# Products that pile up in PSUM, VectorE for the late remainders, and additions made by the DMA queue, in a hybrid decoder layer

## The chip, the core and the metric

The kernel runs on one core of one Trainium2 chip. The core has a matrix engine (TensorE: PE in the profile for its matmuls, PEld for the loads of its weights), a vector engine (VectorE: DVE), an engine for activations and copies (ScalarE: ACT), a general engine (GpSimd: POOL), and a queue engine (SyncE: SP) that issues the DMAs. Matmuls add into PSUM, a small memory in banks of 128 partitions x 512 float32; everything else works on SBUF, 128 partitions wide. The metric is the device time of one execution in microseconds (us), lower is better.

## The reference

One decoder layer for 1024 tokens and a width of 1024, all in float32: a norm, one wide projection that feeds two branches (sliding-window attention with 16 heads, and gated linear attention with 4 heads), each branch gated and projected, the two results merged with sigmoid gates, one output projection, the residual, and a norm at the end.

```python
h = rms_norm(x, norm_w)
z = h @ w_in                      # q, k, v, gates of both branches, merge gates m_a, m_b
o_a = sliding_window_attention(...) * silu(gate_a)
o_b = rms_norm(gated_linear_attention(...)) * silu(gate_b)
y = sigmoid(m_a) * (o_a @ w_a_proj) + sigmoid(m_b) * (o_b @ w_b_proj)
out = rms_norm(x + y @ w_out, final_norm_w)
```

## The kernel before, in words

**Float32 on a matrix engine that takes less.** Every operand of a matmul is held in two parts of the reduced format fp32r: the rounded value `h` and the remainder `l`. A product of two operands is three matmuls, h·h + h·l + l·h. For weights, `split_w` (L114-116) makes `h` by a copy on ACT (L115) and `l` by a subtraction on POOL (L116). For data, `split_block` (L878-880) makes `h` on ACT (L879) and `l` on DVE, or on POOL where the caller says so (L880).

**Seven products instead of eight.** A 1024-deep product is cut into 2 x 2 blocks and computed by Winograd's form of Strassen's scheme, `seven_products` (L398-463): seven half products of sums of the blocks of weights (a11, a12, a21, a22) with sums of the blocks of data (b11, b21, t4, t2, t3, t1, b22), and then additions of the seven results into the four blocks of the output. We call the products by their factors: P1 = a11·b11, P2 = a12·b21, P3 with t2, P4 with t1, P5 with t3, P6 with t4, P7 with b22. Each product has PSUM banks of its own, and DVE does the additions: seven for every output tile (L426, L436, L462). Before P3, four subtractions on DVE make the sums of the weights (L454-457), and each of the seven weights goes through `split_w`.

**Stages.** Norm and transposes of x (to about 100 us of the profiled span); the projections for the merge gate m_b, for q, k, v and the gate of the linear branch, in pairs of 128 or 256 columns through `seven_products` (100 to 440); the attention (440 to 740); the linear branch together with the remaining projections, and the projection of the first branch, `ya`, whose gated result t1 goes to HBM as `sp_t1` (740 to 922); then the **end stage**, in which the second branch is projected and merged, and the layer's output is made.

**The end stage.** The output of the second branch, `sp_ob`, is loaded (tiles `r`) and turned into the seven data blocks `ob` (`b0` to `b9` and `o0` to `o3`, each an `h` and an `l`). Four steps k = 0 to 3 follow, each a `seven_products` of 7 x 12 matmuls of 128x512 with a pair of column blocks of `w_b_proj`; `merge` takes each of the four output tiles c11, c12, c21, c22, multiplies it by the gate (L957), and adds the part of the first branch that it loads from `sp_t1` (tile `yt`, L958). The sixteen merged tiles stay in SBUF (`mg`). When all four steps are through, `block_sums` makes the seven data blocks of the merged result, `mt`: 16 sums on DVE (L891-L898) and 28 splits. Of the splits' remainders DVE takes those of blocks 2 and 3, POOL those of blocks 0, 1, 4, 5 and 6. The output projection is two `seven_products` with n = 256 (h = 0 and 1, each half of the 1024 output columns), 7 x 48 matmuls of 128x256 each (L395). `residual` loads the piece of x that belongs to a tile (`xr`) and DVE adds it (L1000); `norm` has ACT sum the squares (L1007), and POOL multiply by the final norm's weight (L1011). At the very end `finish` scales by the root and stores.

**What sets the order.** The program states what depends on what. A scheduler that simulates a timeline then puts each engine's instructions into one fixed list. An engine takes its own list in order: an instruction that waits holds up all that stand behind it on that engine. Names with a number in the listings below are tiles; a tile that reuses the space of another one waits for it.

Of the kernel before, what the change touches and what calls it, by code (L numbers as in the profile page):

```python
# [69 lines left out]
def layer_kernel(ctx: ExitStack, tc: tile.TileContext, consts, x, positions, norm_w, w_in, a_sinks,  # L70
# [42 lines left out]

    def split_w(raw, h, l):  # L114
        nc.scalar.copy(h, raw)  # L115
        nc.gpsimd.tensor_sub(l, raw, h.bitcast(F32))  # L116
# [10 lines left out]
    def half_product(p, w, m, start, stop):  # L127

        for k in range(4):
            with tc.issue_after(pace.pop(0)) if pace else nullcontext():  # L130
                for y, (a, b) in enumerate(((w[0], m[0]), (w[0], m[1]), (w[1], m[0]))):
                    nc.tensor.matmul(p, a[:, k, :], b[:, k, :], start=start and k == 0 and y == 0,  # L132
                                     stop=stop and k == 3 and y == 2)
# [257 lines left out]
    def token_product(p, w, m, t):  # L391

        for k in range(4):
            for y, (i, j) in enumerate(((0, 0), (1, 0), (0, 1))):
                nc.tensor.matmul(p, m[i][:, k, t * P : t * P + P], w[j][:, k, :], start=k == 0 and y == 0,  # L395
                                 stop=k == 3 and y == 2)

    def seven_products(raw, tset, n, u_pool, dest, emit, early=None, fine=False):  # L398
# [7 lines left out]

        def product(raw, m):
            w = part(raw, n)
            x = [bank("sj") for b in range(nb)]
            for b in range(nb):  # L410
                if n == P:
                    half_product(x[b], w, m, True, True)
                else:
                    for t in range(2):
                        token_product(x[b][:, t * 256 : t * 256 + 256], w, m, 2 * b + t)
            return x

        def tiles(name):
            return [u_pool.tile([P, 512], F32, name=name) for b in range(nb)]
# [4 lines left out]
        def add(o, u, x):  # L424
            for b in range(nb):
                nc.vector.tensor_add(o[b], like(u[b], o[b]), like(x[b], o[b]))  # L426

        def earlier(u, a, th):
            for b in range(nb):
                if early:  # L430
                    early(u[b], a, th, b)

        def give(a, th, u, x):
            o = [dest(a, th, b) for b in range(nb)]
            for b in range(nb):
                nc.vector.tensor_add(o[b], like(u[b], o[b]), like(x[b], o[b]))  # L436
                emit(o[b], a, th, b)

        x = product(a11, b11)
        u = tiles("u")  # L440
        for b in range(nb):
            nc.scalar.copy(u[b], x[b])
        x = product(a12, b21)
        c = [dest(0, 0, b) for b in range(nb)]
        add(c, u, x)
        earlier(c, 0, 0)
# [595 lines left out]
```

## Time and profile before

| | |
|---|---|
| three timed runs | 1125.82, 1119.82, 1123.76 us (median 1123.76) |
| the profiled execution's own time | 1122.67 us |
| its span, and what lies around it | 1120.8 us, 1.87 us |
| matmuls in the profile | 5544 |
| mean granted clock of TensorE | 0.969 |
| end stage: from the last matmul of `ya` to the last matmul | 921.85 to 1111.4 us |
| after the last matmul | 9.4 us |

Busy time is the sum of the durations of an engine's instructions. Where an engine idles, the profile names what ended the wait ("releaser"). The start-to-start time of two instructions that follow each other is called pitch here: it is what one more instruction of a kind costs an engine that never waits, and it is shorter than an instruction's own duration, since neighbours overlap.

### The profile page before, as it was taken

Reading aid. Unit: us, or ns where it says so; the run is one execution under the profiler, and the core shown is the slowest. Engines: PE = TensorE matmul, PEld = TensorE weight load, DVE = VectorE, ACT = ScalarE, POOL = GpSimd, SP = SyncE. Lnnn points to the kernel's source line nnn. Section 1 sums busy time; section 2 is a strip of 40 time slices with the busy share of each in tenths; the row PEclk is TensorE's granted clock in tenths of the full one; section 3 lists DMA queues with packets and bytes.
Section 4 is the critical chain, followed back from the end, with each engine's and each line's share of the span. In section 5 each row is a group of like instructions: output and inputs, shape, how many; then the busy total and the mean of one; then the engine's idle time right before and its main releaser. Section 6 shows DMA issues by size and latency. Waiting matters only on the chain.

```text
span 1120.8 us, 16315 instructions
## 1 busy us (share of the span) xinstructions
PE 1035.0 (92%) x5544; PEld 877.8 (78%) x5544; DVE 765.8 (68%) x1225; ACT 542.4 (48%) x1312; POOL 705.5 (63%) x558
## 2 busy tenths in 40 slices
PE   4797999989999999999999999988999998994896
PEld 3575878868889997888888888776788876874896
DVE  6894687554565422378888888748765199899766
ACT  6326576333343222466666665647554144243444
POOL 4544555677788354867677768548735244688685
PEclk8998999999999999999999999999899998997999
DMA  6303433544333325212222223356644587531315
GB/s 230 95 29 118 149 124 123 169 136 150 101 113 105 112 75 133 72 46 82 67 83 71 64 67 103 109 196 227 197 144 155 167 264 251 180 113 56 121 50 188
DMA packets 126403, 141.07 MB, mean 126 GB/s; under 512 B 10352, under 2 KB 87024, under 8 KB 126320
## 3 DMA queue, kind: packets, MB, share of 16 engines
q1 hardware_dynamic: 126320, 140.03, 39.7%
q8 instruction: 44, 0.72, 0.3%
q14 instruction: 39, 0.32, 0.1%
HBM read 95.04 MB, written 40.24 MB: 121 GB/s over the span
## 4 chain that ended last, share of the span: by engine, by line
PE 57%; DVE 14%; POOL 10%; issue 6%; DMA 5%; ACT 5%; SPq 2%; POOLq 0%; DVEq 0%; ACTq 0%
PE sj L132 21%; PE pj L132 15%; PE sj L395 11%; POOL wl L116 3%; POOL b L880 2%; PE av L748 2%; PE av L703 1%; PE sc L663 1%; DMA r<-sp_ob 1%; POOL o L880 1%; DVE qa L643 1%; ACT sm L678 1%; POOL q L585 1%; DMA oraw<-sp_oa 1%; PE sc L748 1%
## 5 line engine op out<-in xcount | busy, mean ns | idle before, releaser
L132 PE MATMUL pj<-o,wh 128*128 128x512 f32 x1088 | 357.9, 404 | 10.4 <-DVE low L308 6.0
L132 PEld LDWEIGHTS pj<-o,wh 128*128 128x128 f32 x1088 | 203.5, 192 | 53.7 <-issue 6.4
L116 POOL TENSOR_TENSOR wl<-wr,wh 128x1024 fp32r<-128x1024 f32 (+1 forms) x76 | 166.9, 2206 | 98.0 <-ACT wh L115 85.9
L132 PE MATMUL pj<-o,wl 128*128 128x512 f32 x544 | 217.6, 400 | 0.0
L116 POOL TENSOR_TENSOR wl<-sraw,wh 128x512 fp32r<-128x512 f32 (+1 forms) x98 | 152.6, 1574 | 90.6 <-ACT wh L115 80.9
L132 PEld LDWEIGHTS pj<-o,wl 128*128 128x128 f32 x544 | 103.9, 191 | 22.1
L132 PE MATMUL sj<-o,wh 128*128 128x512 f32 x352 | 112.0, 399 | 4.8 <-ACT wh L115 4.8
L115 ACT CAST wh<-wr 128x1024 fp32r<-128x1024 f32 (+1 forms) x76 | 67.0, 890 | 92.1 <-PE pj L132 24.4
L426 DVE TENSOR_TENSOR u<-u,sj 128x512 f32<-128x512 f32 x72 | 49.2, 684 | 74.2 <-PE sj L395 38.3
L115 ACT CAST wh<-sraw 128x512 fp32r<-128x512 f32 (+1 forms) x98 | 63.3, 678 | 63.3 <-PE sj L395 27.9
L132 PEld LDWEIGHTS sj<-o,wh 128*128 128x128 f32 x352 | 66.7, 190 | 21.5 <-ACT wh L115 5.1
L395 PE MATMUL sj<-wh,b 128*128 128x256 f32 x320 | 62.5, 297 | 21.4 <-ACT b L879 14.4
L395 PEld LDWEIGHTS sj<-wh,b 128*128 128x128 f32 x320 | 53.0, 204 | 22.8 <-ACT b L879 14.8
L132 PE MATMUL sj<-o,wl 128*128 128x512 f32 x176 | 70.1, 398 | 0.0
L695 POOL TENSOR_TENSOR ch<-ph,cst 128x512 fp32r<-128x512 f32 x32 | 38.4, 1199 | 46.9 <-ACT ph L694 34.4
L678 ACT ACTIVATE sm<-sc,nm 128x129 f32<-128x129 f32 x128 | 45.8, 368 | 36.7 <-DVE nm L674 35.6
L132 PE MATMUL sj<-b,wh 128*128 128x512 f32 x160 | 51.4, 405 | 4.3 <-ACT wh L115 4.3
L395 PE MATMUL sj<-wh,o 128*128 128x256 f32 x320 | 55.2, 277 | 0.1
L395 PEld LDWEIGHTS sj<-wh,o 128*128 128x128 f32 x320 | 48.4, 188 | 0.4 <-ACT wh L115 0.3
L395 PE MATMUL sj<-wl,b 128*128 128x256 f32 x160 | 45.9, 294 | 0.2 <-POOL wl L116 0.2
L395 PE MATMUL sj<-wl,o 128*128 128x256 f32 x160 | 44.2, 277 | 0.0
L583 POOL TENSOR_TENSOR qs<-qs,sin 128x512 f32<-128x512 f32 x18 | 25.0, 1391 | 30.3 <-DMA qs<-q 30.3
(313 smaller groups left out, 2748.7 us busy)
## 6 DMA issues: line engine op xcount, KB each, us to landing
sraw<-in_w_in_dram SPq DMA_DIRECT2D x32, 512.0 KB, 4.0
wr<-in_w_in_dram SPq DMA_DIRECT2D x26, 512.0 KB, 3.9
r<-sp_ob SPq DMA_DIRECT2D x28, 256.0 KB, 4.5
qs<-q SPq DMA_DIRECT2D x72, 64.0 KB, 2.0
xt<-in_x_dram SPq DMA_DIRECT2D x8, 512.0 KB, 8.7
sp_ma<-gt SPq DMA_DIRECT2D x16, 256.0 KB, 2.0
sp_mb<-c SPq DMA_DIRECT2D x16, 256.0 KB, 2.0
gt<-sp_cum SPq DMA_DIRECT2D x16, 256.0 KB, 3.8
```

The costliest lines, as they stand in the source:

```text
L115: nc.scalar.copy(h, raw)
L116: nc.gpsimd.tensor_sub(l, raw, h.bitcast(F32))
L132: nc.tensor.matmul(p, a[:, k, :], b[:, k, :], start=start and k == 0 and y == 0, stop=stop and k == 3 and y == 2)
L395: nc.tensor.matmul(p, m[i][:, k, t * P : t * P + P], w[j][:, k, :], start=k == 0 and y == 0, stop=k == 3 and y == 2)
L426: nc.vector.tensor_add(o[b], like(u[b], o[b]), like(x[b], o[b]))
L583: nc.gpsimd.tensor_mul(qs, qs, sin[:, sl])
L585: nc.gpsimd.tensor_add(q, q, qs)
L643: nc.vector.tensor_sub(qa[64:128, :], r[0:64, :], qa[0:64, :].bitcast(F32))
L678: nc.scalar.activation(sm[:, j, :], sel[j // 2][:, j % 2, :], AF.Exp, bias=nm[:, j : j + 1], accum_out=den[:, j : j + 1])
L695: nc.gpsimd.tensor_mul(ch, ph.bitcast(F32), leb)
L748: nc.tensor.matmul(p, a[i], b[j], start=start and y == 0, stop=stop and y == 2)
L880: (eng or nc.vector).tensor_sub(m[1][:, k, :], r, f(m, 0, k))
```

## The change

- **`seven_products` is rewritten.** P3 and P5 are added by TensorE onto the banks in which P1 stands, P7 onto the banks of P4. After P1, after P3 and after P5, ACT copies the bank out (tiles u1, u3, u5). DVE has four additions for each output tile (`give`, L433 of the changed kernel): c11 = u1 + P2, c22 = u5 + P4, c21 = u5 + P6, c12 = u3 + (P4 + P7). Nothing is added into the bank of P4 until c22 has read it. The weights a11, a12 and a22 are split ahead of the four subtractions. The order of the products is an argument: 1 to 7, or for n = 256 (1, 2, 6, 3, 5, 4, 7) and in the first half of the output projection (1, 2, 4, 6, 3, 5, 7).
- **Remainders.** From the projection of the first branch's fourth column block on, `split_w` makes `l` on DVE (`rest[0] = nc.vector`). All remainders of data blocks and the multiplication by the norm's weight go from POOL to DVE too.
- **Sums earlier.** `block_sums` is gone. The last two of the second branch's data blocks are made between the products of step k = 0, and the seven blocks of the merged result between the products of step k = 3 (`sums`): the parts of k = 0, 1, 2 first, and those of k = 3 as their tiles come.
- **Additions by DMA.** In `merge`, for k < 3, a DMA issued by GpSimd adds `sp_t1` into the tile in SBUF (twelve of 256 KB, L976); for k = 3 the load and DVE's addition stay. The residual is added in the same way for the whole first half and for two of four tile groups of the second (twelve of 256 KB, L1021).
- **Places.** The halves of `w_out`'s rows are exchanged together with the data blocks; some pools lie elsewhere, t2 shares the tiles `r`, and the memory for the queue of GpSimd's DMAs is set to 1024.

```diff
+    rest = [nc.gpsimd]
+
     def split_w(raw, h, l):
         nc.scalar.copy(h, raw)
-        nc.gpsimd.tensor_sub(l, raw, h.bitcast(F32))
+        rest[0].tensor_sub(l, raw, h.bitcast(F32))
...
+        w = {i: part(r, n) for i, r in ((1, a11), (2, a12), (6, a22))}
         nc.vector.tensor_add(a22, a21, a22)
         nc.vector.tensor_sub(a21, a11, a21)
         nc.vector.tensor_sub(a11, a22, a11)
         nc.vector.tensor_sub(a12, a12, a11)
+        by = {1: (b11, a11), 2: (b21, a12), 3: (t2, a11), 4: (t1, a22), 5: (t3, a21), 6: (t4, a22), 7: (b22, a12)}
...
+        def product(i, b):
+            if n == P:
+                half_product(x[i][b], w[i], by[i][0], i not in (3, 5, 7), i not in (1, 3, 4))
...
+        for i in order:
+            if i not in w:
+                w[i] = part(by[i][1], n)
+            x[i] = x[{3: 1, 5: 1, 7: 4}[i]] if i in (3, 5, 7) else [bank("sj") for b in range(nb)]
...
+            if i in (1, 3, 5):
+                u[i] = [u_pool.tile([P, 512], F32, name=f"u{i}") for b in range(nb)]
+                for b in range(nb):
+                    nc.scalar.copy(u[i][b], x[i][b])
+                    if i == 3 and early:
+                        early(u[i][b], 0, 1, b)
+            if i == 2:
+                give(0, 0, 1, 2)
+            if i in (4, 5) and 4 in x and 5 in u:
+                give(1, 1, 5, 4)
+            if i in (5, 6) and 6 in x and 5 in u:
+                give(1, 0, 5, 6)
+            if i == 7:
+                give(0, 1, 3, 7)
+            if after:
+                after(i)
...
     ya_tiles((0, 1, 2))
+    rest[0] = nc.vector
...
             nc.vector.scalar_tensor_tensor(o, m, 1.0, o, ALU.add, ALU.mult)
-            nc.vector.tensor_add(o, o, t)
+            if k < 3:
+                nc.gpsimd.dma_start(o, sp_t1[c : c + P, sl], accum_op=ALU.add)
+            else:
+                t = yw.tile([P, 512], F32, name="yt")
+                nc.sync.dma_start(t, sp_t1[c : c + P, sl])
+                nc.vector.tensor_add(o, o, t)
...
-    block_sums(mt, [(k, [mg[i][th][:, k, :] for i in range(2) for th in range(TH)]) for k in range(4)], zw, (0, 1, 4, 5, 6))
...
-            nc.vector.tensor_add(u, u, xr)
+            if h == 0 or (a, th) in ((0, 0), (0, 1)):
+                nc.gpsimd.dma_start(u, xs, accum_op=ALU.add)
+            else:
+                xr = zw.tile([P, 2, 256], F32, name="xr")
+                nc.sync.dma_start(xr, xs)
+                nc.vector.tensor_add(u, u, xr)
...
-                    nc.gpsimd.tensor_mul(o[:, t, :], o[:, t, :], fnw[:, cs])
+                    nc.vector.tensor_mul(o[:, t, :], o[:, t, :], fnw[:, cs])
```

The instruction lists show what this moves. The first place is POOL, from the projections of the end stage to the first tiles of the output. Before (`wl` is a weight's remainder, the tiles `b_...` and `o_...` on the left are remainders of the blocks `mt`, `o_10208` a tile of the output):

```order
L116 TENSOR_TENSOR wl<-wr,wh 128x512 x26
L880 TENSOR_TENSOR b_10119<-o_9490,b_10118 128x512 x3
L880 TENSOR_TENSOR b_10121<-o_9492,b_10120 128x512 x3
L880 TENSOR_TENSOR b_10119<-o_9490,b_10118 128x512
L116 TENSOR_TENSOR wl<-wr,wh 128x1024 x2
L880 TENSOR_TENSOR b_10127<-o_9491,b_10126 128x512 x3
L880 TENSOR_TENSOR o_10129<-o_9490,o_10128 128x512 x3
L880 TENSOR_TENSOR b_10121<-o_9492,b_10120 128x512
L116 TENSOR_TENSOR wl<-wr,wh 128x1024
L880 TENSOR_TENSOR o_10131<-o_9493,o_10130 128x512 x4
```

After, from the last three tiles of step k = 2 on (`o_9381` to `o_9384` are the merged tiles c11, c12, c21 and c22; `u_...` and `o_10104` on belong to the output):

```order
L976 DMA o_9384<-sp_t_78 128x512
L976 DMA o_9383<-sp_t_78 128x512
L976 DMA o_9382<-sp_t_78 128x512
L1021 DMA o_10104<-in_x_dram 128x2x256 x2
L1021 DMA u_10411<-in_x_dram 128x2x256
L1021 DMA u_10412<-in_x_dram 128x2x256
L1021 DMA o_10105<-in_x_dram 128x2x256
L1021 DMA o_10104<-in_x_dram 128x2x256
```

Nine more lines of the first kind stand ahead of these, and five of the second behind. POOL's subtractions and multiplications are gone from its list in the end stage; what stands there is the issue of 24 DMAs, and at the very end the roots of the final norm.

The second place is DVE, from the last tile of step k = 3 to the sums. Before (`o_9490` to `o_9493` are the merged tiles, `t_...` and `b_...` sums and remainders for the output projection):

```order
L436 TENSOR_TENSOR o_9491<-u,sj 128x512
L957 SCALAR_TENSOR_TENSOR o_9491<-ym,o_9491 128x512
L958 TENSOR_TENSOR o_9491<-o_9491,yt 128x512
L893 TENSOR_TENSOR t_10149<-o_9493,o_9490 128x512
L891 TENSOR_TENSOR o_9490<-o_9491,o_9490 128x512
L894 TENSOR_TENSOR o_9492<-o_9492,t_10149 128x512
L898 TENSOR_TENSOR o_9491<-o_9493,o_9491 128x512
L880 TENSOR_TENSOR b_10125<-t_10149,b_10124 128x512
L880 TENSOR_TENSOR b_10123<-o_9492,b_10122 128x512
L893 TENSOR_TENSOR t_10157<-o_9493,o_9490 128x512
```

After, in the same place (`b_9891`, `b_10046` and `o_10080` are remainders of blocks that go into the output projection, `u_9944` is the copy of P3; the additions that give c21 and c22 of k = 3 stand ten rows higher):

```order
L433 TENSOR_TENSOR o_9382<-u_9944,sj 128x512
L866 TENSOR_TENSOR b_10046<-o_9381,b_10045 128x512
L980 TENSOR_TENSOR o_9384<-o_9384,yt 128x512
L118 TENSOR_TENSOR wl<-wr,wh 128x1024
L866 TENSOR_TENSOR o_10080<-o_9382,o_10079 128x512
L980 TENSOR_TENSOR o_9383<-o_9383,yt 128x512
L866 TENSOR_TENSOR o_10080<-o_9382,o_10079 128x512
L974 SCALAR_TENSOR_TENSOR o_9382<-ym,o_9382 128x512
L866 TENSOR_TENSOR o_10080<-o_9382,o_10079 128x512
L412 TENSOR_TENSOR wr<-wr 128x1024
L866 TENSOR_TENSOR b_9891<-o_9383,b_9890 128x512
L980 TENSOR_TENSOR o_9382<-o_9382,yt 128x512
```

Additions out of PSUM, gates, remainders of blocks, sums, and remainders and sums of the weights of the output projection now stand mixed in one list. TensorE's list changes with it: 37 matmuls of the output projection's first two products stand ahead of step k = 3's last product.

The third place is the first tile group of the output, on DVE after the change (`fnw` is the norm's weight, `o_10104` the tile into which the DMA of L1021 adds):

```order
L433 TENSOR_TENSOR o_10104<-u_10185,sj 128x2x256
L433 TENSOR_TENSOR o_10104<-u_10186,sj 128x2x256
L866 TENSOR_TENSOR b_9947<-r,b_9946 128x512
L866 TENSOR_TENSOR b_10015<-o_9384,b_10014 128x512
L866 TENSOR_TENSOR b_10046<-o_9381,b_10045 128x512
L118 TENSOR_TENSOR wl<-wr,wh 128x1024
L1038 TENSOR_TENSOR o_10104<-o_10104,fnw 128x256 x4
L118 TENSOR_TENSOR wl<-wr,wh 128x1024 x2
```

The multiplications of L1038 stand behind the DMAs that add x into the same tile, and two weight remainders stand behind them in the list.

221 lines of the change are left out of this document (103 added, 118 removed).

## The prediction

> **What bounds the kernel now.** I read the page's busy list and its chain first, then the busy time by stage, then what TensorE waited for in the end stage, and last the rows around each wait.
>
> ```profile
> span 1120.8 us, 16315 instructions
> PE 1035.0 (92%) x5544; PEld 877.8 (78%) x5544; DVE 765.8 (68%) x1225; ACT 542.4 (48%) x1312; POOL 705.5 (63%) x558
> PE 57%; DVE 14%; POOL 10%; issue 6%; DMA 5%; ACT 5%; SPq 2%; POOLq 0%; DVEq 0%; ACTq 0%
> ```
>
> TensorE is busy 92% of the span, so only its idle or slow stretches can be won, and the number of its matmuls does not change. By stage (columns: PE, PEld, DVE, ACT, POOL busy with instructions, granted clock, DMA share, GB/s):
>
> ```profile
> 100.00:440.00 340.00, 334.69 (x1761) 285.37 (x1762) 177.90 (x224) 141.74 (x222) 218.12 (x143) 0.99 0.40 126
> 921.85:1004.08 82.23, 77.92 (x329) 63.30 (x328) 75.80 (x86) 30.47 (x52) 53.58 (x35) 0.96 0.62 193
> 1004.08:1050.23 46.15, 24.39 (x155) 22.70 (x153) 43.60 (x40) 17.40 (x29) 33.76 (x18) 0.78 0.13 40
> 1050.23:1111.40 61.17, 61.16 (x518) 60.97 (x518) 41.42 (x58) 27.51 (x76) 49.98 (x43) 1.00 0.38 126
> 1111.40:1120.80 9.40, 0.00 (x0) 0.00 (x0) 3.52 (x12) 3.68 (x8) 3.03 (x7) 0.73 0.60 223
> ```
>
> The hole is 1004 to 1050 us, the hand-over from the second branch's projection to the output projection: 24.39 us busy of 46.15, clock 0.78. From 1050 on TensorE is the bound again, at 61.17 / 518 = 0.118 us per 128x256 matmul. The waits from 880 us on (total, times, longest) and two rows of the chain (start, length):
>
> ```profile
> PE sj L395 <- ACT b L879: 14.4, 2, 12.6
> PE sj L395 <- DVE b L880: 4.8, 2, 3.6
> PE sj L132 <- ACT wh L115: 4.3, 1, 4.3
> PE sj L395 <- DVE u L426: 2.2, 1, 2.2
> PE sj L395 <- POOL wl L116: 0.2, 1, 0.2
> ...
> 925.46 4.97 DMA r<-sp_ob
> 932.69 54.86 PE sj L132 x227
> ```
>
> and TensorE's timeline after the first of these waits (start, length, operation, idle before it):
>
> ```profile
> 932.69 2.08 PE L132 MATMUL sj<-b,wh 128*128 128x512 f32 x4 [4.31 <-ACT wh L115]
> 938.31 0.40 PE L132 MATMUL sj<-b,wl 128*128 128x512 f32 x1
> ```
>
> Thirteen matmuls take the 5.62 us between these two rows; in the chain's run of 227, with the excess taken off, one takes (54.86 - 2.6) / 227 = 0.23, and 13 would be 3.0. So a long wait costs 2.6 us more in slow clock. The end stage after `ya` runs from 921.85 to 1111.40, 189.55 us. Its matmuls alone, 334 of 128x512 and 672 of 128x256, need 334 x 0.23 + 672 x 0.118 = 156.1. **Lost: 33.4 us** = 4.3 + 2.6 at the start, 21.6 of waits in the hand-over (14.4 + 4.8 + 2.2 + 0.2), and the remaining 4.9 in slow clock there. Nothing outside of this is large: the pairs stage, with 334.69 busy of 340.00, can give 5.3 at most.
>
> **The change, part by part.**
>
> *Start of the second branch's projection.* ACT's weight copy stood behind a data split that waited for a load of 4.97 us. The last two data blocks now come inside step k = 0, so the weight copy stands ahead of them, and the wait moves to P4, which needs a block whose loads are queued on SP behind the last stores of `ya`. My walk gives 1.5 us there, between 0 (loads early) and 3 (a load of 4.97 begun two microseconds before it is needed). In place of 6.9: **-5.4**.
>
> *The hand-over.* Before, the sums and splits for the output projection were done by POOL and DVE after the last step. What they cost, and how they slow each other (groups of the end stage from 880 us: busy, mean ns; then DVE's timeline with and without POOL beside it):
>
> ```profile
> L116 POOL TENSOR_TENSOR wl<-wr,wh 128x512 fp32r<-128x512 f32 x28 | 44.4, 1603 | 33.6 <-ACT wh L115 27.6 <-DMA sp_t<-yt 4.9 <-DMA ym<-sp_mb 1.1
> L116 POOL TENSOR_TENSOR wl<-wr,wh 128x1024 fp32r<-128x1024 f32 x16 | 42.6, 2672 | 29.6 <-ACT wh L115 29.6
> L880 POOL TENSOR_TENSOR b<-o,b 128x512 fp32r<-128x512 f32 x12 | 20.6, 1741 | 0.0
> L1011 POOL TENSOR_TENSOR o<-o,fnw 128x256 f32<-128x256 f32 x24 | 21.9, 937 | 2.8 <-ACT zj L1007 2.8
> L958 DVE TENSOR_TENSOR o<-o,yt 128x512 f32<-128x512 f32 x16 | 19.5, 1218 | 0.7 <-DMA yt<-sp_t 0.4
> L442 ACT COPY u<-sj 128x512 f32<-128x512 f32 x8 | 4.7, 584 | 3.5 <-PE sj L395 3.2 <-PE sj L132 0.3
> ...
> 1030.35 1.75 DVE L880 TENSOR_TENSOR b<-o,b 128x512 fp32r<-128x512 f32 x1
> 1032.02 1.76 DVE L893 TENSOR_TENSOR t<-o,o 128x512 f32<-128x512 f32 x1
> 1035.19 0.69 DVE L880 TENSOR_TENSOR b<-o,b 128x512 fp32r<-128x512 f32 x1
> 1035.80 0.69 DVE L893 TENSOR_TENSOR t<-o,o 128x512 f32<-128x512 f32 x1
> 1036.52 0.69 DVE L894 TENSOR_TENSOR o<-o,t 128x512 f32<-128x512 f32 x1
> 1044.32 1.28 DVE L426 TENSOR_TENSOR o<-u,sj 128x512 f32<-128x512 f32 x2
> 1045.51 1.22 DVE L457 TENSOR_TENSOR wr<-wr 128x1024 f32<-128x1024 f32 x1
> 1046.65 1.28 DVE L1000 TENSOR_TENSOR o<-o,xr 128x512 f32<-128x512 f32 x2
> ```
>
> Beside POOL's subtractions a DVE addition starts every 1.67 us (1030.35 to 1032.02). Alone, the pitch is 0.61 for 128x512 (1035.19 to 1035.80), 0.72 where the next one needs the result (1035.80 to 1036.52), and 1.14 for 128x1024 (1045.51 to 1046.65). So taking some 1.7 to 2.7 us of POOL's time off per remainder costs DVE 0.6 to 1.14, and frees DVE's other rows of their slow pace. DVE still has more to do in one place. I walk both lists from t0, the moment at which TensorE ends P5 of step k = 2. By the lists DVE does 60 operations of 128x512 and 4 of 128x1024 from there to the remainder of block b11's part of k = 3 (`b_9891`), the last thing that the first product of the output projection needs: 60 x 0.60 + 4 x 1.14 = 40.6. Its head waits for ACT's copy of P5 (0.58 by the row of L442 above) and its end takes 0.69: 41.9, and my walk, with a short wait for a later product between, has 42.4. TensorE's list to the same place holds 98 matmuls of 128x512 and 80 of 128x256: 98 x 0.23 + 80 x 0.118 = 31.9. It therefore loses 10.5 us on the way, however the waits are spread, and by my walk 0.9 at two later splits: 11.4. One long wait costs 2.6 of clock on top: 14.0 in place of 21.6 + 4.9 = 26.5: **-12.5**. After that 491 matmuls are left, 58 us, in which DVE has about 44 us of work at the same pitches: TensorE is the bound.
>
> *DVE's dependent rows.* The walk used the pitch of independent rows. If a third of its 64 rows wait for the one ahead, 0.11 each: **+2.5**; 0 if the list is mixed well, 7 if all are.
>
> *Additions by DMA.* Twelve additions of L958 (1.2 us each) and twelve of L1000 leave DVE, and SP's loads go with them; those additions are already out of the count above. No DMA issued by POOL, and none that adds, is in the trace. The nearest rows are loads of the same size on SP's queue (KB, us to landing) and, from above, a load of twice the size with much else under way:
>
> ```profile
> yt<-sp_t SPq DMA_DIRECT2D x16, 256.0 KB, 3.7
> xr<-in_x_dram SPq DMA_DIRECT2D x16, 256.0 KB, 3.0
> r<-sp_ob SPq DMA_DIRECT2D x28, 256.0 KB, 4.5
> xt<-in_x_dram SPq DMA_DIRECT2D x8, 512.0 KB, 8.7
> ```
>
> A plain load could be issued early; an addition cannot begin until its tile is multiplied by the gate, so its whole latency lies between that row and the tile's first reader. Two places are tight. For c21 of k = 2, nine DVE rows cover it, 9 x 0.60 = 5.4. For the first tile of the output, three rows and a 128x1024 cover two such DMAs, 2.9, and L1038's four multiplications wait for them with the next weights' remainders behind them; those have some 5 us before TensorE wants them. At 3.0 to 4.5 nothing of it reaches TensorE but the second of two in a row; I take 4.5 and **+1.5**. At 8.7 it is 3.3 at the first place, 0.8 at the second and about 1 at each of two later tiles, +6; below there is nothing to gain.
>
> The Trainium skill ("DMA: Bandwidth & Descriptors", section Anatomy of one DMA) gives for a DMA issued from GpSimd about 2.0 us plus the bytes over 436 KB per us, an estimate of 2.6 us for 256 KB, less than every row above; by it this term would be 0 and the time 1107; no row shows such a DMA.
>
> *The pairs stage.* Of seven DVE additions per tile four are left, 24 tiles in the whole program: 72 of 0.69 us fewer, and 24 ACT copies more. DVE is busy 177.90 of 340 us there and ACT 141.74, so TensorE hides both. New are three waits per pair: P3, P5 and P7 write onto banks that ACT or DVE must have read. One product of twelve matmuls (12 x 0.23 = 2.8 us) stands between each reader and its writer, and a copy and an addition take 0.6 + 0.69 = 1.3. Cost **0**, between -5.3 (the stage's holes vanish, since DVE has fewer rows) and the rival below.
>
> *Tail.* The 9.40 us behind the last matmul keep their last product, addition, squares, root and stores: 0.
>
> Sum against the profiled execution: 1122.67 - 5.4 - 12.5 + 2.5 + 1.5 = 1108.8, **1109 us**. That execution is 1.1 below the median of the runs shown, less than their spread.
>
> **The rivals.**
>
> *DVE keeps ahead (1095).* The scheduler's list for DVE may start earlier than my t0 in its cheap parts, and hide the 10.5. Then only the start's 1.5 and the DMAs' 1.5 are left of 33.4, and some 2 of clock: 1122.67 - 33.4 + 5 = 1094. For it: POOL no longer slows DVE, and DVE is busy only 75.80 of 82.23 us before the hole even at the slow pace. Against: 64 rows stand between two fixed points, and none of them is idle time.
>
> *The shared banks bite in the pairs stage (1123).* ACT and DVE take their lists in order; where a weight's copy (0.62) and a 128x512 sum at 1.67 beside POOL, which in this stage keeps its remainders, stand ahead of the reader, 1.3 becomes 3.6, and the writer waits 0.8 to 1. One such wait in each of 14 pairs is 14 us: 1109 + 14 = 1123. For it: POOL is busy 218.12 of 340 there. Against: ACT is busy 42% and DVE 52%, and the lists I walked for three pairs leave 1 to 5 us of slack.
>
> *The DMAs that add land late (1131).* Mechanism: an ACT or DVE instruction that reads the tile stands in the list and holds up the weights' parts behind it. From 12 us on it decides: 12 - 5.4 = 6.6 for c21 of k = 2, 12 - 2.9 - 5 = 4.1 for the first output tile, and about 4 at each of three later tiles, 22.7 in place of 1.5: 1109 + 21 = 1130 to 1131, slower than before. For it: each is one transfer of 128 rows that has to read, add and write, and all share one queue. Against: 3.0 to 4.5 for the plain ones, and 0.13 of DMA share in the hand-over.
>
> The Trainium skill ("SBUF — State Buffer", "Who interferes with whom") warns that DMAs issued from GpSimd starve while DVE runs some operations, because their descriptors cannot be written; it takes additions of two SBUF tensors out of that, by inference. DVE's list in this place is of such additions, so by the exception nothing happens, and by the warning this rival's 1131 would come. No row of this trace decides it.
>
> **How the numbers follow.** What a measurement of this kernel can tell from no change is about 0.5%: under 1118.1 is faster, over 1129.4 slower. The forecast, DVE bounding the hand-over, 1102 to 1118: 0.55. DVE ahead, 1090 to 1102: 0.12. Pairs stage, 1115 to 1129: 0.20, of which 0.07 under 1118. Late DMAs: 0.13, of which 0.10 above 1129.4. Faster 0.55 + 0.12 + 0.07 = 0.74; slower 0.10 and 0.01 for both losses together, 0.11; same 0.15. The range leaves out 0.07 below and 0.12 above: 1094 to 1126. Its upper end is 1109 plus 4.5 for dependent rows, 4.5 for DMAs at 8.7 and 8 of the pairs' 14; its lower end the first rival.
>
> **What would show it.** In the changed profile: a wait of 1 to 3 us, not 4.3, where the second branch's projection starts; waits on DVE remainders (`b`, `wl`) of 10 to 13 us in all around step k = 3's last product and the start of the output projection, where 21.6 stood, and the stretch from `ya`'s last matmul to the last matmul of all at about 175 us; DVE rows at 0.6 to 0.7 with POOL quiet; DMAs from POOL that land in 3 to 5 us; 100 to 440 us within 2 us of its old length. I am wrong if POOL's DMAs show more than 8 us, if TensorE's waits in the pairs stage name `u` or `c` in many small pieces, or if the hand-over holds no wait on DVE above 2 us.

## The result, and the profile after

The changed kernel takes **1132.55 us** in the median (1131.14 to 1134.62), the kernel before beside it 1124.05: a ratio of 1.0078, 95% interval 1.0051 to 1.0106. It is slower by 0.8%, where 1109 was forecast, with a range of 1094 to 1126. The profiled execution took 1131.14 us, with these lines on its page (span; busy time; share of the chain that ended last; then GpSimd's DMA queue, with packets, MB and share):

```profile
span 1129.4 us, 16128 instructions
PE 1046.2 (93%) x5544; PEld 881.4 (78%) x5544; DVE 705.4 (62%) x1224; ACT 557.2 (49%) x1340; POOL 568.9 (50%) x487
PE 42%; DVE 17%; issue 14%; POOL 9%; DMA 8%; ACT 6%; SPq 1%; POOLq 0%; DVEq 0%; ACTq 0%
...
q0 software_dynamic: 4992, 6.29, 3.6%
```

The work went where the change sends it: POOL 705.5 to 568.9 us, DVE 765.8 to 705.4 although it took over POOL's remainders, ACT 15 more. But the chain's share of TensorE fell from 57 to 42%, and "issue" rose from 6 to 14%. By stage:

```profile
100.00:440.00 340.00, 333.45 (x1741) 279.69 (x1742) 139.15 (x176) 153.66 (x240) 206.64 (x140) 0.99 0.39 124
925.15:1003.00 77.85, 74.79 (x316) 59.34 (x315) 57.43 (x94) 32.11 (x59) 9.79 (x11) 0.98 0.67 176
1003.00:1042.00 39.00, 29.43 (x183) 27.15 (x182) 39.00 (x57) 16.87 (x26) 2.12 (x2) 0.82 0.31 87
1042.00:1120.05 78.05, 66.77 (x508) 65.10 (x507) 38.40 (x70) 30.60 (x83) 17.24 (x21) 0.91 0.45 98
1120.05:1129.40 9.35, 0.04 (x1) 0.00 (x0) 3.54 (x12) 3.52 (x8) 3.20 (x7) 0.78 0.62 228
```

The hand-over (1003 to 1042) is better than it was, with DVE busy 39.00 of 39.00 us: it bounds this stretch, as forecast. The stretch after it is new. Before, 518 matmuls filled 61.17 us without a gap; here 508 take 78.05 with a clock of 0.91. TensorE's timeline in it:

```profile
1054.99 0.80 PE L397 MATMUL sj<-wh,b 128*128 128x256 f32 x2 [3.90 <-ACT u L447]
1085.22 0.80 PE L397 MATMUL sj<-wh,b 128*128 128x256 f32 x2 [4.76 <-ACT wh L117]
1102.23 0.50 PE L397 MATMUL sj<-wh,o 128*128 128x256 f32 x2 [1.44 <-ACT wh L117]
```

Each names a copy on ACT. ACT itself stood behind squares (L1034) that waited for the residual DMAs, on its timeline:

```profile
1047.79 0.42 ACT L1034 ACTIVATE zj<-o 128x256 f32<-128x256 f32 x1 [6.95 <-DMA o<-in_x_dram]
...
1052.47 0.42 ACT L1034 ACTIVATE zj<-o 128x256 f32<-128x256 f32 x1 [3.62 <-DMA o<-in_x_dram]
```

And POOL, which only issues them (start, length, idle before it):

```profile
971.88 1.74 POOL L976 DMA_DIRECT2D o<-sp_t  x2 [7.61 <-DVE o L974]
...
1039.62 1.23 POOL L1021 DMA_DIRECT2D o<-in_x_dram  x1 [34.34 <-issue]
1048.11 1.22 POOL L1021 DMA_DIRECT2D o<-in_x_dram  x1 [7.25 <-issue]
...
1065.93 1.20 POOL L1021 DMA_DIRECT2D o<-in_x_dram  x1 [3.30 <-DVE wl L118]
1070.41 1.22 POOL L1021 DMA_DIRECT2D o<-in_x_dram  x1 [3.29 <-issue]
1075.01 1.20 POOL L1021 DMA_DIRECT2D o<-in_x_dram  x1 [3.39 <-issue]
1079.46 1.22 POOL L1021 DMA_DIRECT2D o<-in_x_dram  x1 [3.25 <-issue]
```

The second residual DMA is ready with the first, at 1039.5 us (both tiles came from one pair of DVE additions), and is issued at 1048.11, just after the first has landed and ACT starts on it (1047.79). Later ones follow each other at 4.5 us, just over the 4.2 us that each of them takes to land; the first took 8.1. The merge's DMAs were issued two at a time (971.88, x2). Something lets one residual DMA at a time through. The residual DMA has 256 rows of 1 KB where the merge's has 128 of 2 KB, and the change gave the memory for this queue the number 1024.

To compare stretches I add up by how much each row of TensorE's timeline starts later than the one ahead allows (0.228 us for each 128x512 matmul, 0.1135 for each 128x256; only excesses over 0.15 us): waits and slow clock together, called **late time** here.

| late time, us | before | changed | forecast for it |
|---|---|---|---|
| pairs stage, 106 to 430 | 6.7 | 10.3 | as before |
| start of the second branch's projection | 7.1 | 6.1 | 1.5 |
| hand-over | 26.5 | 13.9 | 14.0 |
| output projection behind it | 0 | 16.7 | 1.5 |

### The profile page after: what moved, and what is told of

Read it like the earlier page. It is cut to its first block, busy times and chain, and to the rows that moved or that the text cites. A ratio compares the mean times of both kernels' runs of the same rounds, so it can differ in the third digit from the quotient of the medians.

```text
span 1129.4 us, 16128 instructions
## 1 busy us (share of the span) xinstructions
PE 1046.2 (93%) x5544; PEld 881.4 (78%) x5544; DVE 705.4 (62%) x1224; ACT 557.2 (49%) x1340; POOL 568.9 (50%) x487
## 4 chain that ended last, share of the span: by engine, by line
PE 42%; DVE 17%; issue 14%; POOL 9%; DMA 8%; ACT 6%; SPq 1%; POOLq 0%; DVEq 0%; ACTq 0%
PE pj L134 15%; PE sj L134 13%; PE sj L397 7%; POOL wl L118 3%; PE av L737 2%; PE av L692 1%; ACT sm L667 1%; DVE qa L632 1%; DMA r<-sp_ob 1%; DVE qb L633 1%; ACT wh L117 1%; PE sc L652 1%; DMA qs<-q 1%; POOL c L521 1%; DVE sc L660 1%
## 5 line engine op out<-in xcount | busy, mean ns | idle before, releaser
L118 POOL TENSOR_TENSOR wl<-sraw,wh 128x512 fp32r<-128x512 f32 (+1 forms) x98 | 147.2, 1522 | 110.1 <-ACT wh L117 104.2
L433 DVE TENSOR_TENSOR c<-u,sj 128x512 f32<-128x512 f32 x64 | 42.5, 683 | 115.4 <-ACT u L447 50.3
L118 POOL TENSOR_TENSOR wl<-wr,wh 128x1024 fp32r<-128x1024 f32 x29 | 73.0, 2519 | 23.6 <-ACT wh L117 19.4
L397 PE MATMUL sj<-wh,b 128*128 128x256 f32 x320 | 67.9, 311 | 16.0 <-ACT wh L117 6.5
L397 PEld LDWEIGHTS sj<-wh,b 128*128 128x128 f32 x320 | 57.1, 218 | 18.0 <-ACT wh L117 7.4
L976 POOL DMA_DIRECT2D o<-sp_t x12 | 10.7, 932 | 114.5 <-DVE wl L118 57.3
L447 ACT COPY u<-sj 128x512 f32<-128x512 f32 x72 | 41.5, 580 | 53.2 <-PE sj L134 34.3
L397 PE MATMUL sj<-wl,b 128*128 128x256 f32 x160 | 49.5, 312 | 3.1 <-DVE wl L118 3.1
```

Of the source, the lines that this page charges most:

```text
L118: rest[0].tensor_sub(l, raw, h.bitcast(F32))
L433: nc.vector.tensor_add(o, like(u[i][b], o), like(x[j][b], o))
L447: nc.scalar.copy(u[i][b], x[i][b])
```

## The experiments

Every ratio below is against the kernel before, from the same chip.

**The queue's memory.** Two theories for the residual DMAs: the queue's memory holds only one of them, or their own latency and the lists are to blame.

```diff
-    nc = _bacc.Bacc("TRN2", target_bir_lowering=False, num_devices=1, dynamic_dma_scratch_size=1024)
+    nc = _bacc.Bacc("TRN2", target_bir_lowering=False, num_devices=1, dynamic_dma_scratch_size=2048)
```

> The changed kernel with 2048 in place of 1024 for the memory of GpSimd's DMA queue; every engine's list of instructions is the same. Theory (queue memory): in the changed kernel the second residual DMA is issued at 1048.11 us, 8.5 us after the first and only when that one has landed, and the later ones follow each other at 4.5 us, though their tiles are ready; POOL idles 54.8 us ahead of them for 'issue'. Twice the memory lets two be under way: the second is issued within 2 us of the first, the 54.8 fall under 25, TensorE's wait of 3.90 us at 1055 goes and that of 4.76 at 1085 shrinks, with 2.6 of slow clock each: 6 to 12 us less, 1120 to 1127. Rival (the DMAs' own latency, or the lists): the issue times stay as they are or move without effect, 1129 to 1135.

Measured: **1116.49 us**, ratio 0.9955 (0.9932 to 0.9979), 16 us under the changed kernel, with every engine's list unchanged. POOL's timeline now has two and three of these DMAs issued back to back:

```profile
1043.44 2.47 POOL L1021 DMA_DIRECT2D o<-in_x_dram  x2 [34.34 <-issue]
1056.88 1.20 POOL L1021 DMA_DIRECT2D u<-in_x_dram  x1 [10.98 <-ACT u L447]
1058.31 1.20 POOL L1021 DMA_DIRECT2D u<-in_x_dram  x1 [0.23 <-issue]
1061.48 1.19 POOL L1021 DMA_DIRECT2D o<-in_x_dram  x1 [1.97 <-DVE o L433]
1065.07 3.67 POOL L1021 DMA_DIRECT2D o<-in_x_dram  x3 [2.40 <-DVE wl L118]
```

and the output projection is whole again, in the windows by stage:

```profile
1042.00:1108.00 66.00, 65.23 (x548) 64.73 (x546) 42.21 (x76) 31.86 (x84) 18.48 (x22) 1.00 0.58 128
```

Its late time is 0.9 us in place of 16.7. One number in the program's setup cost the change 1.4%. The gain was larger than I expected, since none of the three waits came back.

**Half the size.** The same cause from the other side, at 1024:

```diff
-                nc.gpsimd.dma_start(u, xs, accum_op=ALU.add)
+                for t in range(2):
+                    nc.gpsimd.dma_start(u[:, t, :], xs[:, t, :], accum_op=ALU.add)
```

> Each residual DMA of 256 rows is split into two of 128 rows. Theory (queue memory): a DMA of 128 rows needs half the memory, so two are under way together, as the merge's DMAs were (two issued 0.9 us apart at 971.88); the first token's half lands about 2 us earlier, the last one no earlier: 0 to 6 us less, 1126 to 1132. Rival (each DMA waits for the one before, whatever its size): 24 DMAs in a row at 3 to 4 us each, 5 to 15 us more, 1137 to 1147.

Measured: 1118.15 us, 0.9962 (0.9941 to 0.9982), better than either theory had it. Three of 128 rows are issued at once, then POOL waits 4.82 us:

```profile
1044.70 2.69 POOL L1022 DMA_DIRECT2D o<-in_x_dram  x3 [34.27 <-issue]
1052.21 0.88 POOL L1022 DMA_DIRECT2D o<-in_x_dram  x1 [4.82 <-issue]
```

So the limit is in rows: at 1024 three DMAs of 128 rows go, of 256 rows only one (the profile of the change), and at 2048 at least three of 256 rows go. It is not in bytes: with a fourth half 512 KB would have been under way, and it had to wait, while the two merge DMAs that went together at 1024 (971.88, x2) carry 512 KB in 256 rows.

**Without the residual's DMAs, and without the merge's.**

In `residual` (first run) and in `merge` (second run), so that all goes by load and DVE's addition:

```diff
-            if h == 0 or (a, th) in ((0, 0), (0, 1)):
+            if False:
...
-            if k < 3:
+            if False:
```

> All of the residual by loads and additions on DVE, as before the change; the merge keeps its DMAs. Theory (residual DMAs cost what the forecast missed): TensorE's waits at 1055, 1085 and 1102 us (3.90 + 5.22 + 1.44) and some 5 of slow clock go, DVE has twelve additions of 0.60 more, 7.2 us, of which at most half reach TensorE: 1117 to 1124. Rival (DVE bounds the output projection too): 1131 to 1139.

> The merge by loads and additions on DVE for all k, as before the change; the residual keeps its DMAs. Theory (merge DMAs cost one wait): DVE's idle 2.68 us at 996 and part of the hand-over's waits go, but of twelve additions of 0.60 in the second branch's steps the four of k = 2 stand in the hand-over's list, 2.4 us: 1129 to 1134, no difference that can be told. Rival (the merge's DMAs, 6.2 us to landing, are what slows the end stage): 1118 to 1126.

Measured: `x_loads` 1116.50 us, 0.9942 (0.9917 to 0.9966); `t1_loads` 1136.04 us, 1.0125 (1.0087 to 1.0164). Loads and twelve more additions on DVE are worth as much as the DMAs with enough memory: the DMAs' saving does not reach TensorE. Without the merge's DMAs the changed kernel is 3.5 us slower, a little more than I expected; the two intervals overlap, so that is likely, not shown. In the variant with loads for k = 2 alone, built on a faster kernel below, they made no difference:

```diff
-            if k < 3:
+            if k < 2:
```

> Residual by loads, the pairs stage as before the change, and in the merge of k = 2 the load and DVE's addition in place of the adding DMA (k = 0 and 1 keep it). Theory (the DMAs of k = 2, 6 to 7 us to landing, hold DVE's list at the hand-over by 2.7 us, and four additions of 0.60 cost 2.4): nothing, 1105 to 1109 against 1107.3. Rival (the hand-over's waits come from these DMAs): 3 to 6 us less, 1101 to 1105.

Measured: 1106.36 us, 0.9851 (0.9831 to 0.9872), against 1107.32 of its base.

**The pairs.** TensorE's late time in the pairs grew by half, in small waits; some of them on the changed kernel's timeline:

```profile
170.36 0.49 PE L134 MATMUL sj<-t2h,wh 128*128 128x512 f32 x1 [0.77 <-ACT wh L117]
187.85 0.73 PE L134 MATMUL sj<-o,wh 128*128 128x512 f32 x2 [0.78 <-DVE c L433]
219.95 0.50 PE L134 MATMUL sj<-t3h,wh 128*128 128x512 f32 x1 [0.47 <-ACT u L447]
225.28 0.50 PE L134 MATMUL sj<-o,wl 128*128 128x512 f32 x1 [1.37 <-POOL wl L118]
```

Two of these four name a bank's reader (`c`, `u`), two a weight part. First I undid the pairs' part of the change as a whole, with `seven_old` a copy of the `seven_products` of the kernel before:

```diff
-        seven_products(raw, (b11, b21, t4, t2, t3, t1, b22), n, up_, ..., emit,
-                       range(1, 8) if n == P else (1, 2, 6, 3, 5, 4, 7))
+        seven_old(raw, (b11, b21, t4, t2, t3, t1, b22), n, up_, ..., emit)
```

once with 2048 for the queue (`oldpairs_ring`), once at 1024 with the residual by loads (`oldpairs_x`).

> The changed kernel with 2048 for the DMA queue's memory, and the pairs stage (100 to 430 us) by the seven products as they were before the change: own banks, seven additions on DVE. Theory (waits on shared banks slow the pairs): the stage took 321.7 us before and 327.6 to 330 in the changed kernel and its variants; it returns to 321 to 323, and the whole is 5 to 8 us faster than the 1116.5 with 2048 alone: 1108 to 1112. Rival (the stage's length differs for another reason, the order of the weight parts or the place of the tiles): no more than 2 us won, 1114 to 1118.

> The queue's memory at 1024, the residual by loads and additions on DVE, the pairs stage as before the change. Theory (the two losses are independent): 1116.5 of the loads alone less 5 to 8: 1108 to 1112. Rival (pairs not to blame): 1114 to 1118.

Measured: 1109.08 us, 0.9887 (0.9871 to 0.9903), and 1107.32 us, 0.9866 (0.9847 to 0.9885): 7.4 and 9.2 us less. The old form differs from the new in two ways, its own banks and its order of products, in which P6 with the unsummed a22 comes third and P3, the first with a sum, fourth. Each of them alone, first own banks in the new order (the seven additions on DVE are in a copy of the function, left out here), then shared banks in the old order:

```diff
-            x[i] = x[{3: 1, 5: 1, 7: 4}[i]] if i in (3, 5, 7) else [bank("sj") for b in range(nb)]
+            x[i] = [bank("sj") for b in range(nb)]
...
-                       range(1, 8) if n == P else (1, 2, 6, 3, 5, 4, 7))
+                       (1, 2, 6, 3, 5, 4, 7))
```

> 2048 for the queue's memory; in the pairs stage the changed kernel's order of products and of weight parts, but each product has banks of its own and DVE makes seven additions. It tells two causes of the pairs' longer stage apart. Theory A (waits on the shared banks): the stage goes from 327.6 back to about 322 us, the whole to 1109 to 1112. Theory B (the second to last factors: P3 now comes third instead of fourth, so the weights' sums, and a22's split ahead of them, are due one product earlier): the stage stays at 326 to 329 and the whole at 1114 to 1118.

> 2048 for the queue's memory; in the pairs stage the shared banks of the change, but the products in the order 1, 2, 6, 3, 5, 4, 7 of the kernel before. P5 then follows P3 directly and waits for ACT's copy of the bank (0.6 us and the queue ahead of it), P7 follows P4 and waits for an addition (0.7). Theory A (shared banks): twelve pairs with about 1.3 us or more each, 15 us more than the 327.6 of the stage, 1128 to 1136. Theory B (the weights' order): the stage falls to 322 to 325 and the whole to 1110 to 1114.

Measured: `ownbanks` 1119.60 us, 0.9967 (0.9952 to 0.9982); `sharedold` **1109.27 us**, 0.9875 (0.9849 to 0.9901). The order is the cause, the banks are not. With the queue's memory at 2048 in all four, one profile of each gives (us; the pairs from their first matmul to their last, which varies by 2.6 us in three profiles with one list of TensorE):

| | median | pairs | from the pairs' start to `ya`'s last matmul | from there to the last matmul |
|---|---|---|---|---|
| shared banks, new order (`ring2048`) | 1116.49 | 327.8 | 825.6 | 179.6 |
| own banks, new order (`ownbanks`) | 1119.60 | 336.8 | 832.7 | 172.8 |
| shared banks, old order (`sharedold`) | 1109.27 | 318.0 | 823.0 | 174.6 |
| own banks, old order (`oldpairs_ring`) | 1109.08 | 322.8 | 823.4 | 174.2 |

In the pairs themselves the new order costs 9.8 us with shared banks and 14.0 with own ones, while sharing saves 9.0 and 4.8. What TensorE waited for in the pairs, of `ownbanks` and then of `sharedold` (total, times, longest):

```profile
PE sj L134 <- ACT wh L117: 11.4, 4, 5.7
PE pj L542 <- DVE u L547: 2.3, 2, 1.8
```

```profile
PE sj L134 <- POOL wl L118: 1.0, 1, 1.0
PE sj L134 <- ACT wh L117: 0.3, 1, 0.3
```

All four of the first kind in `ownbanks` stand at the start of P3 (data `t2h`), the first product with a summed weight, and where the longest ends, ACT's copy of that weight has waited for the sum (L484, the third of DVE's four there):

```profile
207.02 0.80 PE L134 MATMUL sj<-t2h,wh 128*128 128x512 f32 x1 [5.73 <-ACT wh L117]
206.35 0.62 ACT L117 CAST wh<-sraw 128x512 fp32r<-128x512 f32 x1 [2.24 <-DVE sraw L484]
```

So the new order makes these sums due one product earlier than DVE has them. With shared banks in the old order, P5 right behind P3 and P7 right behind P4 in the program, no wait on a copy or an addition is left in the pairs, and their late time is 2.1 us, less than the 6.7 before the change. My expectation of 1.3 us for each pair was wrong: the scheduler puts other products' matmuls between. How the gain reaches the end is only partly a matter of the pairs. Of the 9.8 us, 2.6 are left at `ya`'s last matmul, since the stretch between takes 7.2 longer. Over the profiles of the change and its variants that point lies 825.4 to 829.4 us after the pairs' start in the seven with the changed pairs and 821.1 to 825.3 in the seven with the old order, 5.0 apart in the mean. The rest comes in the end stage, whose start has 1.1 us of late time in `sharedold` where `ring2048` has 7.1; a new order of the pairs makes new lists for all that follows.

**The two losses together.** The order alone, at 1024, and both losses away, the residual by loads:

```diff
-                       range(1, 8) if n == P else (1, 2, 6, 3, 5, 4, 7))
+                       (1, 2, 6, 3, 5, 4, 7))
```

> The changed kernel with one edit: the pairs' products in the order 1, 2, 6, 3, 5, 4, 7, the queue's memory left at 1024. Theory (the two losses add): 7 us less than the 1132.5 of the change, 1123 to 1128, with TensorE's waits behind the residual DMAs as large as in the change. Rival (one hides the other): 1129 to 1134 or under 1120.

> The pairs in the old order with shared banks, and the residual by loads: no GpSimd DMA but the merge's twelve. Theory (the adding DMA of the residual is worth nothing even with enough memory): as the 1109.3 with 2048, 1106 to 1111. Rival (twelve additions on DVE cost their 7 us): 1113 to 1117.

Measured: `order1024` 1123.06 us, 1.0008 (0.9990 to 1.0027), 9.5 under the change; `order_x` 1105.49 us, 0.9849 (0.9826 to 0.9871). Together the two are worth 27.1 us, alone 16 and 7 to 9.5, so they add up within 4. Whether the waits behind the DMAs in `order1024` are as large as in the change stays open: no profile of it can be compared with that one.

**The start of the projection.** Two tries at the 5.4 us that did not come: the product that needs the late block sixth instead of fourth, and the two last blocks ahead of step k = 0 again, as before the change.

```diff
-                       ..., merge, range(1, 8), after={0: last_blocks, 3: sums}.get(k))
+                       ..., merge, (1, 2, 3, 6, 5, 4, 7) if k == 0 else range(1, 8), after=...)
...
+    for i in (1, 2, 3):
+        last_blocks(i)
...
-                       ..., after={0: last_blocks, 3: sums}.get(k))
+                       ..., after={3: sums}.get(k))
```

> 2048 for the queue's memory; in step k = 0 of the second branch's projection the order of the products is 1, 2, 3, 6, 5, 4, 7, so that the product that needs the late block comes sixth and not fourth. Theory (loads of that block set the waits at 932 to 948 us, 2.8 us and some 3.7 of slow clock): the waits shrink to the one that P7 then has on the addition behind P4, about 1.3: 2 to 5 us less than 1116.5, 1111 to 1115. Rival (the waits only move to the blocks behind, or P7's wait costs as much): 1115 to 1119.

> As the run with the pairs in the old order and the residual by loads, but the last two data blocks of the second branch are made ahead of step k = 0 again, as before the change. Theory of the forecast (moving them into k = 0 won 5.4 us): 3 to 7 us more, with the wait of about 4 us on ACT's weight copy back at the stage's start. Rival (nothing was won there, the same loads are waited for in both): the same within 2 us.

Measured: `late4` 1116.57 us, 0.9954 (0.9937 to 0.9970), as its base; `early_blocks` 1105.65 us, 0.9842 (0.9823 to 0.9860), as its base `order_x`. Neither moves anything, and in `early_blocks` the start has no wait of 4 us either. But its base has a quiet start already, so it shows only that the place of these blocks does not matter there. The traces show what does: in the changed kernel, where the start is not quiet, ACT's split waits for a load of `sp_ob`, and TensorE for the split:

```profile
939.65 1.66 ACT L865 CAST o<-r 128x512 fp32r<-128x512 f32 x3 [5.23 <-DMA r<-sp_ob]
940.84 0.50 PE L134 MATMUL sj<-o,wh 128*128 128x512 f32 x1 [1.12 <-ACT o L865]
```

The last four of these loads land 14.3 to 16.4 us after `ya`'s last matmul here and 14.3 to 16.3 in `late4`; in `sharedold` three of the four have landed by 11.4 and the last at 14.2, and in `ownbanks`, which has the new order and a quiet start too (1.3 us of late time), all by 8.2. That points to the place of these loads in SP's list; an edit of it alone was not run.

**The order in the second branch's steps.**

```diff
-                       ..., merge, range(1, 8), after=...)
+                       ..., merge, (1, 2, 6, 3, 5, 4, 7) if k < 3 else range(1, 8), after=...)
```

> As the run with the pairs in the old order and the residual by loads, and the old order in steps k = 0 to 2 of the second branch's projection too. Theory (the order costs what the weights' sums make late, here too): 1 to 4 us less than that run. Rival (DVE makes the remainders in these steps, so the order's cost does not arise; P5 and P7 then wait on banks): the same within 2 us, or up to 5 more.

Measured: **1102.61 us**, 0.9820 (0.9782 to 0.9858): 1.8% faster than the kernel before and the fastest of all; against `order_x` the intervals overlap, so the last 2.9 us are likely, not shown. Its hand-over still waits for DVE, in the list of waits from 910 us on:

```profile
PE sj L397 <- DVE b L866: 4.4, 1, 4.4
PE sj L397 <- ACT b L865: 2.0, 1, 2.0
PE sj L397 <- ACT wh L117: 1.7, 1, 1.7
```

**The remainders alone, on either side.** The kernel before with nothing but its POOL work of the end stage moved to DVE (`only_dve`), and the change with 2048 and the output projection's weight remainders back on POOL (`wpool`, the last two lines):

```diff
-        nc.gpsimd.tensor_sub(l, raw, h.bitcast(F32))
+        rest[0].tensor_sub(l, raw, h.bitcast(F32))
...
-            split_block(tset[i], k, r, nc.gpsimd if i in onpool else nc.vector)
+            split_block(tset[i], k, r)
...
-                    nc.gpsimd.tensor_mul(o[:, t, :], o[:, t, :], fnw[:, cs])
+                    nc.vector.tensor_mul(o[:, t, :], o[:, t, :], fnw[:, cs])
...
     zw = lctx.enter_context(pool_of(name="zw", bufs=2, side="right"))
+    rest[0] = nc.gpsimd
```

In `only_dve`, `rest[0] = nc.vector` stands behind `ya_tiles((0, 1, 2))`, as in the change.

> The kernel before the change with one part of it alone: all remainders of the end stage and the norm's multiplication on DVE instead of POOL; products, sums, merge and residual as before. Theory (DVE with POOL quiet beside it does both engines' work in less time than the two did together): the hand-over, 26.5 us of waits and slow clock, has some 16 sums, 28 remainders and 8 weight sums and remainders on DVE, 16 x 0.60 + 28 x 0.60 + 8 x 1.14 = 35.5, of which before the change DVE and POOL had at 1.67 to 2.7 each: 0 to 8 us less, 1115 to 1124. Rival (POOL was a real help): 1126 to 1136.

> 2048 for the queue's memory; the remainders of the output projection's fourteen weights are made on POOL again, all else on DVE. Theory (DVE bounds the hand-over, and POOL's subtractions beside it slow it): four of them, 4 x 1.14 = 4.6 us, leave DVE's list in the hand-over, and during four times about 2.5 us of POOL its rows start every 1.67 and not 0.60 us, which gives 6.4 back; later POOL's DMAs wait behind the remainders: 1115 to 1122, no gain. Rival (only the length of DVE's list counts): 4 to 7 us less, 1109 to 1113.

Measured: `only_dve` 1117.14 us, 0.9952 (0.9931 to 0.9973), its hand-over's late time 17.9 in place of 26.5; `wpool` 1126.47 us, 1.0036 (1.0019 to 1.0053), 10 us over its base. The theory's sign holds in both, but `wpool` is 4 us slower than its range, and by another mechanism. While DVE's list is dense, DVE keeps its pace and POOL does not, on DVE's and then POOL's timeline:

```profile
1009.20 1.29 DVE L936 TENSOR_TENSOR o<-o,r 128x512 f32<-128x512 f32 x2
1010.41 1.29 DVE L866 TENSOR_TENSOR b<-r,b 128x512 fp32r<-128x512 f32 x2
1011.61 0.69 DVE L866 TENSOR_TENSOR o<-o,o 128x512 fp32r<-128x512 f32 x1
...
1012.82 1.28 DVE L433 TENSOR_TENSOR o<-u,sj 128x512 f32<-128x512 f32 x2
1014.01 1.65 DVE L866 TENSOR_TENSOR b<-o,b 128x512 fp32r<-128x512 f32 x1
```

```profile
1004.91 10.20 POOL L118 TENSOR_TENSOR wl<-wr,wh 128x1024 fp32r<-128x1024 f32 x1 [11.95 <-ACT wh L117]
1015.06 0.87 POOL L976 DMA_DIRECT2D o<-sp_t  x1
1015.67 2.66 POOL L118 TENSOR_TENSOR wl<-wr,wh 128x1024 fp32r<-128x1024 f32 x1
```

One remainder takes POOL 10.20 us beside DVE's dense list and 2.66 without it, a merge DMA stands behind it, and TensorE waits 14.0 us in all for POOL's remainders. POOL's remainder gets through when DVE comes to an addition out of PSUM (L433, with one operand in SBUF where the rows around it have two): this one ends 2.3 us after such a row starts, the three others in the hand-over 2.3 to 2.6 after one, and each time the DVE row behind it takes 1.65 to 2.5 us in place of 0.69.

## Why the prediction was wrong, step by step

- **Additions by DMA, "+1.5".** This step failed. The place was named (the first output tile, ACT's and DVE's lists held behind it), and the latency of one DMA was inside the bounds taken, 3.0 to 8.7 us: 4.2 in the median for the residual's and 6.2 for the merge's. The very first residual DMA, the one at the tight place, took 8.1, just above the 8 that the prediction named as a sign of being wrong; loads on SP's queue were under way beside it, and the DMA engines' busy share was 0.58 or more from 1041 to 1048 us. With twice the memory it took 8.0, and next to nothing of it reached TensorE. What was not seen is that one could not be issued before the last had landed. "All share one queue" stood in the rival without a price, beside "one transfer of 128 rows" where the residual's have 256, and the setting of 1024 stood in the list of changes. The term measured 16.7, and 0.9 with twice the memory. The sum took the DMAs one by one, and a queue has to be asked how many it holds.
- **The rival of late DMAs, 1131, 0.13.** Its time was met within 2 us by luck, through a mechanism next to it: tiles late by a queue in front of the issue, not by 12 us of landing.
- **The pairs stage, "0".** Failed too. The rival named shared banks at 14 us; the stage lost 3.6 us of late time and `ya`'s end came 4.4 later after the stage's start. Waits that name `u` or `c`, the rival's sign, are 1.6 of 5.8 us there. Undoing the banks gave nothing, undoing the order 7.2. The step counted the additions and the waits on banks, and passed over that the weights' sums and their splits are due one product earlier.
- **The hand-over, "-12.5".** Right: 13.9 us of late time left, 14.0 forecast, and DVE busy without a gap from 1003 us on. TensorE's waits up to `b_9891` are 9.6 us: 4.6 name DVE and 5.0 ACT, whose copy in the longer of two (3.3) stood behind a DVE addition. From DVE's first addition behind P5 of k = 2 to the end of `b_9891` it is 43.5 us (984.91 to 1028.4), 42.4 by the walk; 2.7 of it is the wait for the merge's DMA.
- **DVE's dependent rows, "+2.5".** Nothing: DVE's rows start every 0.60 us all through the hand-over, since the list is mixed well.
- **Start of the projection, "-5.4".** 1.0 came. The loads for the last two blocks were still waited for: the walk had the risk ("a load of 4.97 begun two microseconds before it is needed"), but the last four of them land 14 to 16 us after `ya`'s end, behind what it took. The start is quiet in the kernels with the old order of pairs and the new end stage (late time 0.8 to 2.1), and in `ownbanks` with the new order, wherever these loads stand earlier. Why the scheduler puts them earlier there stays open.
- **Tail.** 9.35 us, as forecast.

The sum of the differences: 15.2 for the DMAs, 4.6 for the start, 4.4 ahead of `ya`'s end, less 0.1, 2.5 and the 1.1 us by which the pairs began earlier: 20.5 of the 22.3 us between 1108.8 and 1131.14. The rest is of the size of the excesses under 0.15 us, which the late time leaves out. With the two edits that take the failed steps away the kernel comes to 1105 to 1109, where the forecast was; that the number is met is partly luck, since the start and the pairs differ from what the sum took.

The Trainium skill's fit ("DMA: Bandwidth & Descriptors", Anatomy of one DMA), an estimate of 2.6 us for 256 KB, is under everything measured here: 4.2 to 4.5 us in the median for the residual's and 6.2 for the merge's. Its warning that such DMAs starve beside DVE ("SBUF — State Buffer", Who interferes with whom) does not show here: at 1004.40 us, with DVE busy without a gap, the issue of one took POOL 0.88 us, as elsewhere, and it landed after 5.2. That agrees with the page's exception for additions of two SBUF tensors, which it calls inferred.

## What to carry to other kernels

A DMA that adds replaces a load that could be early by a transfer that cannot, so its latency and the number of them that the queue holds at once are on the path; look at the queue's memory against the rows of one transfer before costing any of them. When a block of work is put into a new order, list for every product which operand is due earlier than it was, not only which waits are new. And giving an idle POOL subtractions beside a dense list of DVE can make them four times as long, so what is waited for must not be among them.

## What the runs showed of the hardware

- At 1024 for the queue's memory one adding DMA of 256 rows of 1 KB is under way at a time, or three of 128 rows; at 2048 at least three of 256 rows. So 384 rows went at 1024 and 512 did not. POOL shows the wait ahead of the residual's DMAs as idle time put down to "issue", 54.8 us in the changed kernel and 34.6 at 2048, of which 34.3 is the time before the first.
- Beside a dense list of DVE rows with two operands in SBUF (0.60 us each; `wpool`) a POOL subtraction of 128x1024 took 10.20 us and two took 13.80, against 2.40 to 2.66 where nothing held it up. DVE kept 0.60 until its next addition out of PSUM; there POOL got through, and the DVE row behind took 1.65 to 2.5 us. In the kernel before, both were slow row by row: 1.67 us on DVE, 1.74 on POOL for 128x512; which of the two happens is not shown. Spans on POOL are rough, but the wait of 6.77 us that TensorE had for the remainder of 10.20 is not.
